# Forget-gate bias rows shifted once per block position, and score steps issued three ahead, in a gMLP and forgetting-attention trunk on Trainium2

## The chip, the cores and the metric

The kernel runs on one core of one Trainium2 chip. The metric is the device time of one launch in microseconds (us). The kernel before takes 2192.91 us, the median of three runs (2192.88 to 2193.39). TensorE (PE) does the matmuls, VectorE (DVE), ScalarE (ACT) and GpSimd (POOL) the elementwise work, and SyncE (SP) issues nearly all DMAs. Each engine works through its own instructions strictly in the order in which they were placed.

## The reference, cut to what matters

One gMLP layer, then one layer of forgetting attention with 12 heads over 1024 positions, each followed by a convolutional FFN. The change lies in the forgetting attention:

```python
f_logit = kvf[..., 2 * TOK_WIDTH:] + b_f
log_f_cum = jnp.cumsum(jax.nn.log_sigmoid(f_logit), axis=1)      # (b, s, 12)
...
for i in range(s // Q_BLOCK):                                    # Q_BLOCK = 128
    q0, q1 = i * Q_BLOCK, (i + 1) * Q_BLOCK
    logits = einsum("bqhd,bkhd->bhqk", q[:, q0:q1], k[:, :q1]) * scale
    decay = c[:, :, q0:q1, None] - c[:, :, None, :q1]
    logits = where(qpos >= kpos, logits + decay, -inf)
    p = softmax(logits)
    outs.append(einsum("bhqk,bkhd->bqhd", p, v[:, :q1]))
```

The term that depends on the query alone cancels in the softmax. The kernel therefore needs only the key term, one row of length 1024 per head, less any constant of the query block.

## The kernel before

Matrices are held as a high and a low part, and each product is three matmuls. The attention layer stands at about 1030 to 1440 us of the profiled execution.

**Steps.** The 48 steps are pairs of a head and a block position `jp` (0 to 3); a step has two query blocks of 128 (`a` = 0, 1) and looks at up to 256 x (`jp` + 1) keys. Heads come in pairs, in the order of `PSEQ` = 4, 5, 0, 1, 2, 3, eight steps for each pair. `s_tasks` makes a step's probabilities: it loads the head's row of cumulated log gates from DRAM (`cdram`), spread over 128 partitions, into a tile `nb` (three buffers); DVE takes the negative of one element (`ncq`, L1354); POOL adds it to the whole row (L1355) and adds the causal mask for the last 256 keys (`md`, L1357). PE multiplies queries and keys into a PSUM bank (`pa`), DVE adds the bias, writes the tile `P` and takes the minimum (L1381), ACT takes the exponential (L1387), DVE the reciprocal of the sum (L1388), POOL normalises (L459). `p_tasks` transposes the probabilities on PE into `pc` banks, splits them (ACT `PTh`, DVE `PTl`, L346 and L347), and multiplies them with V.

**Order.** `strict` pins every matmul to the order of the program. The loop over `t` merges `p_tasks` of step t with `s_tasks` of step t + `LOOK`, and puts between them matmuls of "fills": the K, Q and V projections of the next head pairs, each with a step by which it must be done. The rate at which fills are spent is the largest that any deadline asks for; the Q projections of the fourth and of the sixth pair (`PSEQ[3]`, `PSEQ[5]`) have the deadlines 8 x 2 + `KQD` = 21 and 8 x 4 + `KQD` = 37, as the K projections before them. What is left of a fill at its deadline is issued at once. Before the loop, `LOOK` steps of scores are issued, and then `PRE` (10000 ns of modelled PE time) of the first K projection.

**Banks and tiles.** `pa` has six PSUM banks, `pc` two. A score bank is free again when DVE has read it (L1381). A projection needs two `pa` banks from its first matmul to its evacuation. The tile `P` has six buffers, so three steps of two tiles fill them.

**Weights.** A weight block is loaded by SP into `wr` (L184, two buffers), multiplied by a norm's gain on DVE (L213), cast to its high part on ACT (`wh`, L217, two buffers), and its low part taken by POOL, or by DVE for the first four blocks (`wl`, L218). A new load waits until L218 has read the old block. After a Q projection, DVE scales each half of it (`qf`, L447), ACT casts (L429), DVE subtracts (L430), and SP copies the high and the low part to the other 64 partitions (L431, L432); a score matmul of that head pair needs these copies.

**The scan.** Just before the steps, DVE cumulates the log gates of all 12 heads (`cum`, L1532), and SP stores the 12 rows to `cdram` (L1533). The tag `nb`, with its three buffers, also serves `cum` and its two inputs `lf` and `zz`.

Of the kernel before, what the change touches and what calls it, by code (L numbers as in the profile page):

```python
# [10 lines left out]
F32 = mybir.dt.float32  # L11
F32R = mybir.dt.float32r
AF = mybir.ActivationFunctionType
ALU = mybir.AluOpType
AX = mybir.AxisListType

P = 128
D = 1024
S = 1024
# [9 lines left out]
QSCALE = -0.125  # L29
WIDE = 4 * 268  # L30
STRICT = True
LOOK = 2
VD = 11
LAG = 2
JORD = (1, 2, 3, 0)
# [24 lines left out]
def kernel(  # L60
# [33 lines left out]
    nc = tc.nc  # L94
# [6 lines left out]
    dp = ctx.enter_context(tc.tile_pool(name="dp", bufs=1, space=bass.MemoryType.DRAM))  # L101
# [6 lines left out]
    pbufs = [4]  # L108
# [4 lines left out]
    def nm(s):  # L113
        uid[0] += 1
        return f"{s}_{uid[0]}"
# [4 lines left out]
    def pa():  # L120
        return psA.tile([P, CH], F32, tag="pa", name=nm("pa"))
# [4 lines left out]
    def small(n, tag="sm", p=P):  # L126
        return sm.tile([P, n], F32, tag=tag, name=nm(tag))[:p]
# [8 lines left out]
    def mm(*a, **k):  # L136
        ins = nc.tensor.matmul(*a, **k)  # L137
        if strict[0]:
            tc.keep_in_program_order(ins)
        return ins  # L140
# [317 lines left out]
    def normalise(p, rinv):  # L458
        nc.gpsimd.tensor_scalar(p, p, rinv, 1.0, ALU.mult, ALU.mult)  # L459
# [57 lines left out]
    def drain(g):  # L517
        for _ in g:
            pass
# [465 lines left out]
    tp = tA.enter_context(tc.tile_pool(name="tA", bufs=2))  # L985
# [214 lines left out]
    tp = tF.enter_context(tc.tile_pool(name="tFa", bufs=4))  # L1200
# [67 lines left out]
    tp = tB.enter_context(tc.tile_pool(name="tB", bufs=2))  # L1268
# [1 line left out]
    otag[:] = ["nb", 3]  # L1270
    ptl[0] = 3
    t2b[0] = 2
    cdram = dp.tile([12, S], F32, name="cdram")
    odram = dp.tile([6 * P, S], F32, name="odram")
    strict[0] = STRICT
    w_q = b_w_q[0]
# [71 lines left out]
    def s_tasks(h, jp):  # L1348
        ks, dh, dl = (q[h % 2] for q in kq[h // 2])
        n2 = 256 * (jp + 1)  # L1350
        nb = tp.tile([P, S], F32, tag="nb", name=nm("nb"), bufs=3)
        nc.sync.dma_start(nb[:, :n2], cdram[h:h + 1, :n2].broadcast_to([P, n2]))
        ncq = small(1, "ncq")
        nc.vector.tensor_scalar(ncq, nb[:, n2 - 256:n2 - 255], -1.0, None, ALU.mult)  # L1354
        nc.gpsimd.tensor_scalar(nb[:, :n2], nb[:, :n2], 1.0, ncq, ALU.mult, ALU.add)  # L1355
        md = tp.tile([P, 2, P], F32, tag="md", name=nm("md"), bufs=1)
        nc.gpsimd.tensor_tensor(  # L1357
            md, nb[:, n2 - 256:n2].rearrange("p (a k) -> p a k", a=2), cmask, ALU.add)
        pts = []
        for a in range(2):  # L1360
            i = 2 * jp + a
            n = (i + 1) * P
            nd = n - P
            qs = slice(i * P, (i + 1) * P)
            p = tp.tile([P, S], F32, tag="P", name=nm("P"), bufs=pbufs[0])
            mn = None
            for k0 in range(0, n, CH):
                nn = min(CH, n - k0)
                nw = max(nn, 256)
                ps = pa()  # L1370
                mm(ps[:, :nw], dh[:, qs], ks[:, k0:k0 + nw], start=True, stop=False)
                mm(ps[:, :nw], dl[:, qs], ks[:, k0:k0 + nw], start=False, stop=True)
                e1 = min(k0 + nn, nd)
                parts = []
                if e1 > k0:
                    parts.append((k0, e1, nb[:, k0:e1]))
                if k0 + nn > nd:
                    parts.append((nd, n, md[:, a, :]))
                for c0, c1, bias in parts:
                    m2 = small(1)  # L1380
                    nc.vector.tensor_tensor_reduce(  # L1381
                        p[:, c0:c1], ps[:, c0 - k0:c1 - k0], bias, 1.0,
                        3.0e38 if mn is None else mn, ALU.add, ALU.min, m2)
                    mn = m2
                yield 2 * nw * 0.422
            rs, ri = small(1), small(1)
            nc.scalar.activation(p[:, :n], p[:, :n], AF.Exp, bias=mn, scale=-1.0, accum_out=rs)  # L1387
            nc.vector.reciprocal(ri, rs)  # L1388
            normalise(p[:, :n], ri)
            pts.append(p)  # L1390
        probs[h, jp] = pts
        if jp == final[h]:
            kq_free.extend(q[h % 2] for q in kq[h // 2])
# [64 lines left out]
    for pr in range(5):  # L1458
        p = PSEQ[pr + 1]
# [28 lines left out]
    H = 12  # L1488
# [41 lines left out]
        nc.scalar.copy(lf[:, b * CH:(b + 1) * CH], pt[:H])  # L1530
    cum = tp.tile([P, S], F32, tag="nb", name="cum", bufs=3)[:H]
    nc.vector.tensor_tensor_scan(cum, lf, zz, 0.0, ALU.add, ALU.add)  # L1532
    nc.sync.dma_start(cdram, cum)  # L1533
    wst.conv(wst.at["mv"] + 4)
    drain(mvg)
    mq = {}
# [25 lines left out]
    cost_of = [880 * (jp + 1) + 700 * (jp + 1) for _, jp in steps]  # L1562
    for t in range(LOOK):
        drain(s_tasks(*steps[t]))
# [4 lines left out]
    for t in range(48):  # L1569
        work, rate = -done, 0.0  # L1570
        for _, ns, _, d in fills:
            work += ns
            rate = max(rate, work / max(sum(cost_of[t:d]), 1))
        sg = s_tasks(*steps[t + LOOK]) if t + LOOK < 48 else iter(())
        pg = p_tasks(*steps[t])
        mg = itertools.islice(mem_g, MPER) if t >= MEMT else iter(())
        for cost in merge(pg, sg, mg):
            debt += cost * rate
            while debt > 0 and fills and fills[0][2] <= t:
                c = next(fills[0][0], None)  # L1580
                if c is None:
                    fills.pop(0)
                    done = 0.0
                else:
                    debt -= c
                    done += c
            if not fills or fills[0][2] > t:
                debt = 0.0
        while fills and fills[0][3] <= t + 1:
            drain(fills.pop(0)[0])  # L1590
            done = 0.0
        if t in (15, 31):
            pv_flush(0)
# [40 lines left out]
    tp = tF.enter_context(tc.tile_pool(name="tFb", bufs=4))  # L1634
# [60 lines left out]
```

## Time and profile before

| | |
|---|---|
| median of three runs | 2192.91 us |
| profiled execution | 2189.55 us |
| its span, first to last instruction | 2187.5 us |
| PE busy | 2121.6 us, 97% of the span |
| DVE busy | 1714.2 us, 78% |
| ACT busy | 1035.7 us, 47% |
| POOL busy | 785.1 us, 36% |
| mean granted TensorE clock | 0.993 |

PE is busy for nearly the whole span, so what counts are the places where it stands idle or runs at a lower granted clock. The chain of work that ended last has a share of 80% on PE. The shares are means over stages that differ: the attention layer is the part where PE idles most, and its stretches are to be read by themselves, by their idle time and by what ended it.

### The profile page before, as it was taken

How to read it: one execution, taken by the hardware profiler on the slowest of the kernel's cores; microseconds unless marked ns; L12 is line 12 of the kernel's file. 1: busy time of each engine (PE TensorE's matmuls, PEld its weight loads, DVE VectorE, ACT ScalarE, POOL GpSimd, SP SyncE). 2: the span in 40 equal slices, each digit the busy share in tenths (PEclk: the TensorE clock that was granted, in tenths of full speed). 3: DMA queues.
4: the chain of work that ended last, by engine and by line, in shares of the span. 5: the costliest groups of instructions: out<-in, count | busy, mean ns of one | idle time of the engine just before them, and what ended most of it. 6: DMA issues, size and time to landing. Idle time of an engine off the chain costs nothing.

```text
span 2187.5 us, 29468 instructions
## 1 busy us (share of the span) xinstructions
PE 2121.6 (97%) x10657; PEld 1784.9 (82%) x10657; DVE 1714.2 (78%) x2550; ACT 1035.7 (47%) x1732; POOL 785.1 (36%) x588
## 2 busy tenths in 40 slices
PE   8999999999999999999999999899999999999998
PEld 7998877888888888888788788778788888888886
DVE  4645658999999899676787776775899999988966
ACT  6562344444444434353565564764544444444433
POOL 2311443444444100231655554435344444420033
PEclk9999999999999999999999999999999999999999
DMA  5411231222222675622433333443222222267463
GB/s 179 104 30 30 77 106 60 87 87 87 87 78 78 224 279 179 202 103 75 121 88 89 91 94 87 115 158 105 70 87 87 78 78 86 78 218 259 148 203 116
DMA packets 221470, 251.94 MB, mean 115 GB/s; under 512 B 10330, under 2 KB 155904, under 8 KB 221324
## 3 DMA queue, kind: packets, MB, share of 16 engines
q1 hardware_dynamic: 220288, 249.62, 36.1%
q8 instruction: 84, 1.38, 0.3%
q10 hardware_dynamic: 1036, 0.43, 0.1%
q14 instruction: 62, 0.51, 0.1%
HBM read 196.49 MB, written 43.04 MB: 109 GB/s over the span
## 4 chain that ended last, share of the span: by engine, by line
PE 80%; DVE 8%; DMA 5%; ACT 4%; issue 2%; POOL 1%; SPq 0%; ACTq 0%; DVEq 0%; POOLq 0%
PE pa L137 72%; PE pc L137 5%; PE pc L143 2%; DMA nb<-cdram 1%; DVE P L1381 1%; DMA X<-xdram 1%; DVE X L347 1%; DMA ro<-hdram 1%; DVE X L430 1%; ACT P L1387 1%; DVE PTl L347 1%; DMA o<-odram 0%; ACT PTh L346 0%; ACT Pm L481 0%; DVE X L800 0%
## 5 line engine op out<-in xcount | busy, mean ns | idle before, releaser
L137 PE MATMUL pa<-X,wo 128*128 128x512 f32 x3696 | 841.9, 389 | 3.7 <-ACT X L346 2.5
L137 PEld LDWEIGHTS pa<-X,wo 128*128 128x128 f32 x3696 | 692.8, 188 | 150.3 <-ACT X L346 4.3
L137 PE MATMUL pa<-X,X 128*128 128x512 f32 (+2 forms) x1868 | 438.9, 378 | 6.9 <-DVE sm L1381 6.0
L137 PEld LDWEIGHTS pa<-X,X 128*128 128x128 f32 x1868 | 339.5, 189 | 75.5 <-DVE sm L1381 8.3
L137 PE MATMUL pa<-X,wh 128*128 128x512 f32 (+1 forms) x1216 | 352.8, 399 | 7.8 <-ACT wh L217 4.0
L641 POOL TENSOR_TENSOR wo<-raw,wo 128x512 fp32r<-128x512 f32 x132 | 210.5, 1595 | 203.9 <-ACT wo L639 176.6
L137 PEld LDWEIGHTS pa<-X,wh 128*128 128x128 f32 x1216 | 219.0, 189 | 53.9 <-ACT wh L217 4.5
L641 POOL TENSOR_TENSOR wo<-ws,wo 128x512 fp32r<-128x512 f32 x88 | 153.3, 1742 | 289.4 <-ACT wo L639 289.4
L799 ACT CAST X<-ro 128x1024 fp32r<-128x1024 f32 (+1 forms) x142 | 131.1, 964 | 173.9 <-DVE ro L807 68.9
L137 PE MATMUL pa<-X,wl 128*128 128x512 f32 (+1 forms) x608 | 194.1, 398 | 0.0
L639 ACT CAST wo<-ws 128x512 fp32r<-128x512 f32 x176 | 108.3, 617 | 176.3 <-PE pa L137 164.8
L639 ACT CAST wo<-raw 128x512 fp32r<-128x512 f32 x132 | 81.8, 620 | 184.9 <-PE pa L137 175.4
L137 PE MATMUL pa<-wh,X 128*128 128x256 f32 (+1 forms) x800 | 168.8, 289 | 0.1
L800 DVE TENSOR_TENSOR X<-ro,X 128x1024 fp32r<-128x1024 f32 (+1 forms) x124 | 145.0, 1198 | 30.4 <-ACT X L799 28.2
L800 POOL TENSOR_TENSOR X<-ro,X 128x1024 fp32r<-128x1024 f32 (+1 forms) x18 | 45.5, 2535 | 339.4 <-ACT X L799 336.6
L218 POOL TENSOR_TENSOR wl<-wr,wh 128x1024 fp32r<-128x1024 f32 (+1 forms) x41 | 103.4, 2522 | 175.0 <-ACT wh L217 175.0
L137 PEld LDWEIGHTS pa<-wh,X 128*128 128x128 f32 x800 | 133.3, 191 | 1.9 <-issue 0.2
L137 PEld LDWEIGHTS pa<-X,wl 128*128 128x128 f32 x608 | 110.3, 189 | 20.2 <-DVE wl L218 0.5
L137 PE MATMUL pa<-wl,X 128*128 128x256 f32 (+1 forms) x400 | 114.3, 286 | 4.4 <-POOL wl L218 3.6
L347 DVE TENSOR_TENSOR PTl<-pc,PTh 128x512 fp32r<-128x512 f32 (+1 forms) x152 | 90.8, 601 | 30.4 <-ACT PTh L346 28.6
L1387 ACT ACTIVATE P<-P,sm 128x128 f32<-128x128 f32 (+3 forms) x96 | 74.7, 778 | 73.9 <-DVE sm L1381 73.4
L459 POOL TENSOR_SCALAR P<-P,sm 128x128 f32<-128x128 f32 (+3 forms) x96 | 77.2, 806 | 86.7 <-DVE sm L1388 77.3
(195 smaller groups left out, 3312.7 us busy)
## 6 DMA issues: line engine op xcount, KB each, us to landing
ro<-hdram SPq DMA_DIRECT2D x67, 512.0 KB
raw<-in_a_ffn_in_dram SPq DMA_DIRECT2D x44, 512.0 KB
hdram<-X SPq DMA_DIRECT2D x44, 512.0 KB
raw<-in_b_ffn_in_dram SPq DMA_DIRECT2D x44, 512.0 KB
ro<-in_a_ffn_out_dram SPq DMA_DIRECT2D x35, 512.0 KB
ro<-in_b_ffn_out_dram SPq DMA_DIRECT2D x32, 512.0 KB
xdram<-X SPq DMA_DIRECT2D x24, 512.0 KB
X<-xdram SPq DMA_DIRECT2D x24, 512.0 KB
```

What stands on the lines that cost most here:

```text
L137: ins = nc.tensor.matmul(*a, **k)
L143: ins = nc.tensor.transpose(*a)
L218: eng.tensor_tensor(lo, raw, f32(hi), ALU.subtract)
L347: nc.vector.tensor_tensor(lo, src, f32(hi), ALU.subtract)
L430: nc.vector.tensor_tensor(dl[e][a, cs], qf[a], f32(dh[e][a, cs]), ALU.subtract)
L459: nc.gpsimd.tensor_scalar(p, p, rinv, 1.0, ALU.mult, ALU.mult)
L639: nc.scalar.copy(h, src)
L641: eng.tensor_tensor(l, src, f32(h), ALU.subtract)
L799: nc.scalar.copy(h, src)
L800: (nc.gpsimd if pool else nc.vector).tensor_tensor(l, src, f32(h), ALU.subtract)
L1381: nc.vector.tensor_tensor_reduce(p[:, c0:c1], ps[:, c0 - k0:c1 - k0], bias, 1.0, 3.0e38 if mn is None else mn, ALU.add, ALU.min, m2)
L1387: nc.scalar.activation(p[:, :n], p[:, :n], AF.Exp, bias=mn, scale=-1.0, accum_out=rs)
```

## The change

1. After the scan, DVE makes four tiles `cj`, one for each block position, with the 12 rows less their value at the first query of that position, and SP stores each to its own 12 rows of a `cdram` that is now 48 rows high. A step loads row 12 x `jp` + `h`, which is already shifted: `ncq` and POOL's addition to `nb` are gone, and `md` is made straight from the loaded row.
2. For `jp` = 0 and 1 the two query blocks' probabilities lie side by side in one tile `P`.
3. `LOOK` is 3: three steps of scores before the loop, and `s_tasks` of step t + 3 in the loop.

```diff
-LOOK = 2
+LOOK = 3
...
-    cdram = dp.tile([12, S], F32, name="cdram")
+    cdram = dp.tile([4 * 12, S], F32, name="cdram")
...
-        nc.sync.dma_start(nb[:, :n2], cdram[h:h + 1, :n2].broadcast_to([P, n2]))
-        ncq = small(1, "ncq")
-        nc.vector.tensor_scalar(ncq, nb[:, n2 - 256:n2 - 255], -1.0, None, ALU.mult)
-        nc.gpsimd.tensor_scalar(nb[:, :n2], nb[:, :n2], 1.0, ncq, ALU.mult, ALU.add)
+        r = 12 * jp + h
+        nc.sync.dma_start(nb[:, :n2], cdram[r:r + 1, :n2].broadcast_to([P, n2]))
...
+        both = None
+        if jp < 2:
+            both = tp.tile([P, S], F32, tag="P", name=nm("P"), bufs=pbufs[0])
         for a in range(2):
...
-            p = tp.tile([P, S], F32, tag="P", name=nm("P"), bufs=pbufs[0])
+            if both is None:
+                p = tp.tile([P, S], F32, tag="P", name=nm("P"), bufs=pbufs[0])
+            else:
+                p = both[:, a * (n - P):a * (n - P) + n]
...
-    nc.sync.dma_start(cdram, cum)
+    for jp in range(4):
+        n2 = 256 * (jp + 1)
+        cj = tp.tile([P, S], F32, tag="nb", name=nm("cj"), bufs=3)[:H, :n2]
+        nc.vector.tensor_scalar(cj, cum[:, :n2], cum[:, n2 - 256:n2 - 255], None, ALU.subtract)
+        nc.sync.dma_start(cdram[12 * jp:12 * jp + 12, :n2], cj)
```

Three places show how the change moves instructions. In the rows, "waits" names the engines or DMA queues on whose semaphores an instruction waits.

DVE from the scan on, before (`wr` are raw weights of the first K and Q projections, `L1381` rows read a score bank):

```order
L1532 SCALAR_TENSOR_TENSOR cum<-lf,zz 12x1024 [waits DVE_49,Activation_49,Pool_49]
L213 TENSOR_TENSOR wr_8395<-wr_8395,norms 128x1024 [waits DMAHW3_49]
L218 TENSOR_TENSOR wl_8594<-wr_8395,wh_8593 128x1024 [waits Activation_49]
L213 TENSOR_TENSOR wr_8397<-wr_8397,norms 128x1024 [waits DMAHW6_49]
L1354 TENSOR_SCALAR ncq_8606<-nb_8604 128x1 [waits DMAHW6_49]
```

The same place in the changed kernel:

```order
L1536 SCALAR_TENSOR_TENSOR cum<-lf,zz 12x1024 [waits DVE_49,Activation_49,Pool_49]
L1540 TENSOR_SCALAR cj_8591<-cum 12x256 [waits DVE_49]
L1540 TENSOR_SCALAR cj_8594<-cum 12x512
L1540 TENSOR_SCALAR cj_8597<-cum 12x768 [waits DMAHW5_49,DVE_49]
L1540 TENSOR_SCALAR cj_8600<-cum 12x1024 [waits DMAHW6_49,DVE_49]
L213 TENSOR_TENSOR wr_8395<-wr_8395,norms 128x1024 [waits DMAHW3_49]
```

Four instructions stand ahead of the first weight's gain, and the third and the fourth wait for a DMA: `cum` holds one of the three `nb` buffers, so they write into the buffers of the first two and wait for their stores.

PE before the loop, before (the last scores of the second step, then the first K projection, whose two banks are 8675 and 8676):

```order
L137 MATMUL pa_8656<-X_7994,X_8174 128x512 [waits PE_49]
L137 MATMUL pa_8656<-X_7994,X_8176 128x512
L137 MATMUL pa_8675<-X_7729,wh_8593 128x512 [waits PE_49,Activation_49]
L137 MATMUL pa_8676<-X_7729,wh_8593 128x512 [waits DVE_49]
L137 MATMUL pa_8675<-X_7730,wh_8593 128x512
```

The same place in the changed kernel (8676 to 8697 are the banks of the third step):

```order
L137 MATMUL pa_8659<-X_7994,X_8176 128x512
L137 MATMUL pa_8676<-X_7994,X_8174 128x512 [waits DMAHW5_49,PE_49,Activation_49]
L137 MATMUL pa_8676<-X_7994,X_8176 128x512 [waits DMAHW2_49]
L137 MATMUL pa_8681<-X_7994,X_8174 128x256 [waits DVE_49]
L137 MATMUL pa_8681<-X_7994,X_8176 128x256
L137 MATMUL pa_8692<-X_7994,X_8174 128x512 [waits DVE_49]
L137 MATMUL pa_8692<-X_7994,X_8176 128x512
L137 MATMUL pa_8697<-X_7994,X_8174 128x256 [waits DVE_49,PE_49]
L137 MATMUL pa_8697<-X_7994,X_8176 128x256
L137 MATMUL pa_8716<-X_7729,wh_8604 128x512 [waits DVE_49,PE_49,Activation_49]
L137 MATMUL pa_8717<-X_7729,wh_8604 128x512 [waits DVE_49,PE_49]
L137 MATMUL pa_8716<-X_7730,wh_8604 128x512
```

Eight score banks stand ahead of the K projection where there were four, and the projection's two banks now come from banks that DVE has to read first.

PE in the changed kernel where the fourth head pair begins (the last rows of its Q projection, 10739 and 10740, a transpose of `P` for another step, one pair of the next K projection, and the first scores of the pair, `pa_10896`):

```order
L137 MATMUL pa_10739<-X_7974,wl_10645 128x512
L137 MATMUL pa_10740<-X_7974,wl_10645 128x512
L143 MATMUL pc_10876<-ident,P_10490 128x128 [waits DVE_49,Pool_49]
L143 MATMUL pc_10876<-ident,P_10533 128x128 [waits Pool_49]
L143 MATMUL pc_10876<-ident,P_10490 128x128
L143 MATMUL pc_10876<-ident,P_10533 128x128
L137 MATMUL pa_10887<-X_7729,wh_10817 128x512
L137 MATMUL pa_10888<-X_7729,wh_10817 128x512 [waits DVE_49]
L137 MATMUL pa_10896<-X_8710,X_8176 128x384 [waits DMAHW2_49,PE_49,Activation_49]
L137 MATMUL pa_10896<-X_8710,X_8177 128x384 [waits DMAHW3_49,DVE_49]
```

SP at that place in the changed kernel (L431 and L432 are the copies of the Q projection):

```order
L1353 DMA nb_11106<-cdram 128x1024 [waits DMAHW7_49,DVE_49,Pool_49]
L1419 DMA odram<-os_10831 64x256 [waits DMAHW0_49,DVE_49]
L184 DMA wr_11158<-in_w_kv_dram 128x4x256 [waits DMAHW1_49,Pool_49]
L431 DMA X_8176<-X_8176 64x512 [waits DMAHW2_49,PE_49,Activation_49]
L432 DMA X_8177<-X_8177 64x512 [waits DMAHW3_49,DVE_49,PE_49]
```

Before, 48 matmuls and transposes stood between the end of this Q projection and these scores; now four transposes and two matmuls do. At the sixth pair both queues read the same way.

## Rows read from the trace of the kernel before

**Rows 1.** Windows: stretch, its length, busy us (and instructions) by engine, granted clock, DMA.
```profile
1050.00:1400.00 350.00, 328.21 (x2064) 286.40 (x2062) 258.00 (x802) 209.47 (x464) 189.04 (x198) 1.00 0.35 93
1400.00:1440.00 40.00, 29.60 (x171) 23.25 (x171) 30.81 (x63) 30.61 (x87) 12.53 (x27) 0.96 0.58 179
```

**Rows 2.** Waits of PE, 1050 to 1400: waiter, releaser, total us, times, longest.
```profile
PE pc L143 <- DVE PTl L347: 6.5, 6, 2.4
PE pa L137 <- DVE sm L1381: 4.8, 5, 2.1
PE pc L143 <- DVE sm L1388: 4.7, 4, 2.2
PE pc L143 <- POOL P L459: 2.2, 2, 1.8
PE pa L137 <- POOL wl L218: 1.9, 2, 1.1
```

**Rows 3.** Waits of PE, 1400 to 1440, the longest.
```profile
PE pa L137 <- DVE sm L1381: 3.3, 1, 3.3
```

**Rows 4.** Groups by line: instruction, count | busy us, mean ns | idle before, releasers.
```profile
L1354 DVE TENSOR_SCALAR ncq<-nb 128x1 f32<-128x1 f32 x48 | 7.0, 150 | 20.7 <-DMA nb<-cdram 20.4
...
L1355 POOL TENSOR_SCALAR nb<-nb,ncq 128x256 f32<-128x256 f32 (+3 forms) x48 | 46.7, 974 | 75.6 <-DVE ncq L1354 67.4 <-DVE sm L1388 7.6 <-issue 0.6
...
L430 DVE TENSOR_TENSOR X<-qf,X 64x512 fp32r<-64x512 f32 x26 | 27.5, 1059 | 0.7
```

**Rows 5.** Timeline of PE: its idle time behind the fourth and the sixth Q projection.
```profile
1216.38 0.52 PE L143 MATMUL pc<-ident,P 128*128 128x128 f32 x3 [2.37 <-DVE PTl L347]
...
1346.87 0.87 PE L143 MATMUL pc<-ident,P 128*128 128x128 f32 x4 [1.97 <-DVE sm L1388]
```

**Rows 6.** Timeline at the front: start, us, engine, line, operation [idle before <- releaser].
```profile
1034.71 1.19 DVE L213 TENSOR_TENSOR wr<-wr,norms 128x1024 f32<-128x1024 f32 x1
1034.81 0.33 SPq L1533 DMA_DIRECT2D cdram<-cum  x1
1036.71 0.83 SPq L1352 DMA_DIRECT2D nb<-cdram  x2
1037.08 1.26 PE L137 MATMUL pa<-X,wh 128*128 128x512 f32 x4 [4.03 <-ACT wh L217]
...
1040.59 0.15 DVE L1354 TENSOR_SCALAR ncq<-nb 128x1 f32<-128x1 f32 x1 [1.17 <-DMA nb<-cdram]
...
1049.15 0.35 DVE L1381 CUSTOM_DVE_ANT_0 P<-pa,md,sm 128x128 f32<-128x128 f32 x1
```

**Rows 7.** Timeline of SP and DVE: a weight load and the gain that waited for it.
```profile
1176.73 0.39 SPq L184 DMA_DIRECT2D wr<-in_w_kv_dram  x1
...
1181.44 1.60 DVE L213 TENSOR_TENSOR wr<-wr,norms 128x1024 f32<-128x1024 f32 x1 [0.83 <-DMA wr<-in_w_kv_dram]
```

**Rows 8.** Timeline of PE: a pair of score matmuls and the next instruction's start.
```profile
1050.85 0.63 PE L137 MATMUL pa<-X,X 128*128 128x512 f32 x2
1051.32 0.62 PE L137 MATMUL pa<-X,wh 128*128 128x512 f32 x2
```

**Rows 9.** Window at the front, columns as in rows 1: granted clock is 0.57.
```profile
1038.00:1042.00 4.00, 3.99 (x12) 2.90 (x11) 2.71 (x4) 2.33 (x2) 1.07 (x1) 0.57 0.87 153
```

**Rows 10.** Timeline where the sixth pair's Q projection ends.
```profile
1339.31 0.69 DVE L447 SCALAR_TENSOR_TENSOR qf<-pa,rb_b 128x512 f32<-128x512 f32 x1
1339.34 0.60 PE L143 MATMUL pc<-ident,P 128*128 128x128 f32 x4
...
1340.20 2.40 POOL L218 TENSOR_TENSOR wl<-wr,wh 128x1024 fp32r<-128x1024 f32 x1 [4.08 <-ACT wh L217]
...
1342.63 0.38 SPq L184 DMA_DIRECT2D wr<-in_b_w_out_dram  x1
...
1343.12 0.53 SPq L431 DMA_DIRECT2D X<-X  x1
...
1343.75 0.54 SPq L432 DMA_DIRECT2D X<-X  x1
```

## Prediction

> **What bounds the kernel now.** I read the windows of the attention stage first, then PE's waits in it, then the timeline at the places where the order moves. From 1050 to 1400 us PE is busy 328.2 of 350 us at full clock while DVE is busy 258 and POOL 189; from 1400 to 1440 it is busy 29.6 of 40 [rows 1]. The change leaves PE's work as it is, so it can win only PE's idle time: 21.8 us, then 10.4. That is not one bottleneck but many short stops, and PE's waits say which: for a transpose bank behind the split on DVE (6.5 us), for a score bank (4.8), for the reciprocal (4.7), for the normalised tile (2.2), for a weight's low part on POOL (1.9) [rows 2], and one of 3.3 us in the tail [rows 3]. Since every matmul is pinned, a matmul that comes too early in the order stops all behind it. That is the danger in issuing scores earlier.
>
> **What is taken away.** 48 `ncq` instructions, 7.0 us of DVE, with 20.7 us in which DVE stood before them for the loaded row, and 48 POOL additions, 46.7 us [rows 4]. Neither engine bounds the stage, so this counts only through PE's stops. A third step of lead gives the chain minimum, exponential, reciprocal, normalise one more step's time. I count as won: the score-bank waits but for the longest, 4.8 - 2.1 = 2.7 us; of the reciprocal waits the two short ones, 4.7 - 2.2 - 2.0 = 0.5 (the 1.97 is in rows 5); the normalise waits, 2.2; the low-part waits, 1.9, since POOL is freer [rows 2, 5]. Together 7.3 us. Not won are the stops of 2.0 to 2.4 us: they follow K and Q projections, where DVE's four subtractions (1059 ns each, L430, [rows 4]) hold up the splits, and the change does not move these. In the tail I take half of the 3.3 us, 1.5 [rows 3], as the last scores are issued a step earlier. Gain: 8.8 us; bounds 3.7 (the low parts and a third of the other 5.4) and 14.9 (the 7.3, the long stops of 2.1 and 2.2 us in rows 2, and all of the tail's 3.3).
>
> **The front, first cost.** (a) Between scan and first gain (L213, at 1034.71) stand four subtractions of 256 to 1024 elements on 12 partitions. The trace has none; the gain on 1024 elements took 1.19 us [rows 6], so I take 0.3, 0.5, 0.7 and 0.9 us by size, bounds half and all of 1.2 per 1024. The third waits for the first one's store. The store before was issued at 1034.81, and the load that waits for it at 1036.71, 1.9 us later [rows 6]. So: first done at 1035.0, store landed at 1037.0, third done at 1037.7, fourth at 1038.6; the first gain starts 3.9 us late. (b) The K projection starts at 1037.08, after an idle 4.03 us [rows 6]. In the new order eight score banks precede it, `pa` has six, and its two banks are those of the second step, free only when DVE has read them. Before, DVE had read the last of these at 1049.15 + 0.35 = 1049.50 [rows 6], which delayed nobody. On DVE two more gains stand inside that chain, and each waits for a weight load that can be issued only when an earlier L218 is done; such a load took 1176.73 to 1181.44, 4.7 us [rows 7]. Shifting the old chain by 3.9 us gives 1053.4. Going through the new order row by row from 1038.6 (gain, cast, low part and gain at 1.2 or a little less each, as the gain in rows 6; the first bank read by 1043.9; the next low part until 1045.5; the first load issued at 1042.0 and landed at 1046.7; gain and three reads of 0.35 us or a little more until 1049.3; the second load issued at 1045.5 and landed at 1050.2; gain and two reads) gives 1052.3; with loads that cost nothing it would be 1051. I take 1052.3. (c) So the K projection starts 15.2 us later. PE has by then done the third step's four score banks, which counts back: a 512-column pair takes 1051.32 - 1050.85 = 0.47 us [rows 8], two such and two of half the size make 1.4. The front costs 13.8 us, bounds 12 and 15.5. Nothing hides it, since the fills, PE's cover, are queued behind. The restart at half clock is paid in both kernels: 0.57 over 4 us, 1.7 us lost [rows 9].
>
> **The fourth and sixth head pair, second cost.** Scores of step t + 3 need the pair's Q copies at t = 21 and 37, the very steps at which that Q projection must be done, and these two fills set the rate, so they end on their deadline. Before there was a step between. Take the sixth pair's end as clock zero (1339.31). Four transposes and a matmul pair, about 0.9 us, are all that PE now has before the scores. The copies went out at +3.8 and +4.4 (1343.12, 1343.75), because SP first issued a weight load (1342.63) that waits for POOL's low part (1340.20 + 2.40) [rows 10]. In the new order a load stands ahead of the copies at both pairs. For their landing, the store of 48 KB took 1.9 us and the first row's load of 128 KB, into as many bytes as a copy, 3.8 to DVE's release at 1040.59 [rows 6]; I take 3.0, between them, as the copies have the longer one's size but read no DRAM. Copies there at +7.4, PE stops for 6.5 us, bounds 5.4 and 7.3. Behind the idle 4.03 us the granted clock was at its lower level of 1.2 GHz for some 3 us, which cost 1.7 us [rows 9]; I add that to each. Against it stand the stops already there, 2.37 and 1.97 us [rows 5], which the longer one swallows, and 1.7 us for the one that had fallen to the lower clock already. Sum: 2 x 8.2 - 6.0 = 10.4 us, bounds 8.2 and 12.0. Nothing in the order fills the stop; the cover was 48 matmuls and transposes.
>
> The shared tile for `jp` 0 and 1 makes four steps in a row need six `P` tiles, seven at three of the changes of head. A seventh waits on DVE for transposes two PE pieces later, so I cost it at nothing; its cover is the three steps of lead, and without it I bound each by the longest score-bank wait, 2.1 us [rows 2].
>
> **Sum.** 13.8 + 10.4 - 8.8 = +15.4 us. The profiled execution took 2189.55 us; it lies 3.4 us under the median, and I apply the difference to the median: 2192.91 + 15.4 = 2208.3 us.
>
> **Rivals.**
> - Q copies in time (0.13): the load ahead of them finds its buffer free, and the scores wait no longer than rows 5 show. For: at the fourth pair the old order had no load there. Against: the new order has, behind the same POOL instruction. 13.8 - 8.8 = +5.0, 2197.9.
> - No front stop (0.08): the K projection finds free banks. Against: six banks, eight tiles ahead. 10.4 - 8.8 = +1.6, 2194.5: the change does little beyond moving waits.
> - Faster (0.05): POOL's 46.7 us and DVE's 27.7 us gone end the long stops too. DVE's subtractions at 1059 ns against 690 for a scaling of twice the partitions [rows 4, 10] look disturbed; if POOL's additions are what disturbs them, all of PE's idle time goes, 21.8 + 10.4 us [rows 1] and two spells at the lower clock, 3.4: 35.6 us. Against it the lower bounds, 12.0 at the front and 2 x 5.4 at the pairs, 22.8: -12.8, 2180.1. It decides once over 22.8 us are won. Against: the instruction beside the long subtractions is POOL's low part (L218), which stays.
> - Dearer (0.12): upper bounds and little gain: 15.5 + 12.0 - 3.7 = +23.8, 2216.7.
>
> By the Trainium skill (SBUF — State Buffer, Who interferes with whom), a VectorE instruction with two SBUF inputs and a GpSimd instruction that reads SBUF block each other, the later one until the earlier ends. By that rule the faster rival's 35.6 us could not all come from POOL's additions, since L218 reads SBUF too; the trace agrees as far as L430's 1059 ns [rows 4] go, and I leave that rival at 0.05.
>
> **How the numbers follow.** Forecast 0.62, own range 2200 to 2216: its bounds all together would give 12.0 + 8.2 - 14.9 = +5.3 and +23.8, but they need not fall together. A measurement of this kernel tells about 0.2%, 4.4 us, from no change. Faster: the faster rival, 0.05. Same: no front stop (0.08) and some of copies in time (0.05), 0.13. Slower: 0.82. The range 2197 to 2218 leaves out no front stop and faster, 0.13, and a little of each edge.
>
> **What would show it.** Right: PE idle for 13 us or more between the last scores and the first K matmul, broken by the third step's scores, with the K projection near 1052; a PE wait on a DMA X<-X of 5 us and more at the fourth and sixth pair, then a granted clock of half for some 3 us; normalise waits nearly gone; POOL 47 us less busy. Wrong: a K start before 1045, pairs without a wait on the copies, or stops behind K projections that shrink below 1 us.

## The result and the profile after

The changed kernel takes 2211.39 us, the median of four runs (2209.49 to 2213.63); the kernel before, measured with it, takes 2192.89 us. The ratio is 1.010, 95% interval 1.0086 to 1.0114. The change makes the kernel slower by 18.5 us; 15.4 were forecast.

The head of the page of the changed kernel's profile, its span and the engines' busy time:

```profile
span 2209.9 us, 29350 instructions
...
PE 2126.8 (96%) x10657; PEld 1792.0 (81%) x10657; DVE 1711.1 (77%) x2506; ACT 1033.8 (47%) x1732; POOL 736.9 (33%) x540
```

The span is 22.4 us longer than in the profiled execution of the kernel before. PE has the same 10657 matmuls. It is busy for 5.2 us more (2121.6 before) and idle for 17.2 us more (2209.9 - 2126.8 = 83.1 against 65.9). POOL has lost 48 us, as the change says, and the kernel is still slower: what was added to PE's waits is larger.

PE's waits from 1044 us to 1440 us (waiter, releaser, total us, times, longest) answer to [rows 2, 3]; the changed kernel's steps end some 20 us later than those of the kernel before, so its tail is in part behind this stretch:

```profile
PE pa L137 <- DVE sm L1385: 19.6, 9, 9.9
PE pa L137 <- DMA X<-X: 15.7, 2, 7.9
PE pc L143 <- DVE PTl L347: 7.8, 10, 2.0
PE pa L137 <- ACT Pm L481: 2.9, 1, 2.9
PE pa L137 <- POOL wl L218: 1.1, 2, 0.8
```

Two lines hold nearly all that is new: score banks behind DVE's reads (L1385), of which most lies at the front, and two waits of a score matmul on the copies of Q (`X<-X`). The waits on the reciprocal (4.7 us in [rows 2]) and on the normalised tile (2.2) are gone, the low part's have fallen from 1.9 to 1.1.

**The front.** DVE's and SP's timeline from the scan on (start, us, engine, line, operation, idle before):

```profile
1034.60 0.74 DVE L1540 TENSOR_SCALAR cj<-cum 12x256 f32<-12x256 f32 x2
1036.45 1.33 DVE L1540 TENSOR_SCALAR cj<-cum 12x768 f32<-12x768 f32 x2 [1.12 <-DMA cdram<-cj]
1037.71 1.21 DVE L213 TENSOR_TENSOR wr<-wr,norms 128x1024 f32<-128x1024 f32 x1
...
1041.34 0.38 SPq L184 DMA_DIRECT2D wr<-in_w_kv_dram  x1
...
1045.86 1.36 DVE L213 TENSOR_TENSOR wr<-wr,norms 128x1024 f32<-128x1024 f32 x1
```

The first gain starts at 1037.71, against 1034.71 in [rows 6]. The third subtraction did wait for a store. The third gain, of a weight block whose load went out at 1041.34, starts at 1045.86, 4.5 us later, and DVE's score reads stand around it. PE's idle places there, from its timeline:

```profile
1043.41 1.22 PE L137 MATMUL pa<-X,X 128*128 128x512 f32 x2 [9.89 <-DVE sm L1385]
1047.64 0.77 PE L137 MATMUL pa<-X,X 128*128 128x256 f32 x2 [3.00 <-DVE sm L1385]
1049.36 0.77 PE L137 MATMUL pa<-X,wh 128*128 128x512 f32 x1 [0.95 <-DVE sm L1385]
1051.43 1.62 PE L137 MATMUL pa<-X,wh 128*128 128x512 f32 x3 [1.30 <-DVE sm L1385]
```

PE waits for a bank four times, 15.1 us in all against 4.03 before. The first two waits are of the third step's scores, the last two of the K projection's two banks, which start at 1049.36 and 1051.43.

**The fourth and the sixth pair.** SP's rows at the fourth pair, then PE's idle places at both:

```profile
1223.16 0.38 SPq L184 DMA_DIRECT2D wr<-in_w_kv_dram  x1
1223.66 0.48 SPq L431 DMA_DIRECT2D X<-X  x1
1224.25 0.53 SPq L432 DMA_DIRECT2D X<-X  x1
...
1228.80 1.09 PE L137 MATMUL pa<-X,X 128*128 128x384 f32 x2 [7.83 <-DMA X<-X]
...
1365.09 1.17 PE L137 MATMUL pa<-X,X 128*128 128x384 f32 x2 [7.91 <-DMA X<-X]
```

These are scores that wait 7.8 and 7.9 us for copies. Before, there were stops of 2.37 and 1.97 us on transposes at these two places [rows 5].

**The clock.** Windows of PE (stretch, length, busy us, granted clock, DMA):

```profile
1043.40:1054.00 10.60, 5.33 (x11) 0.50 0.64 197
...
1260.00:1270.00 10.00, 10.00 (x52) 0.83 0.34 100
1360.00:1370.00 10.00, 4.91 (x18) 0.66 0.68 158
1400.00:1410.00 10.00, 10.00 (x55) 0.83 0.43 113
```

A value between 0.5 and 1 means that the clock changed level inside the window. The lower level (1.2 GHz) is met at the front, behind both long waits (0.86 from 1230 to 1240 behind the first of them), and also near 1260 and 1400, behind stops of 2.1 and 2.0 us, and behind one of 2.9 us at 1425 (0.86 and 0.79 in the two windows from 1420 to 1440).

These windows are of one execution, and the order of the matmuls does not settle the clock. Two of the kernels below, look2 and look2_cj, have their matmuls in the same order, and in both PE stops for 2.4 us up to the same transpose at 1105.64. Behind it the clock fell in the first and not in the second:

```profile
1106.00:1110.00 4.00, 4.00 (x17) 0.61 0.07 16
```

```profile
1106.00:1110.00 4.00, 4.00 (x26) 1.00 0.07 16
```

### The profile page after: what moved, and what is told of

It is laid out like the page before. It is cut to its first block, busy times and chain, and to the rows that moved or that the text cites. A ratio compares the mean times of both kernels' runs of the same rounds, so it can differ in the third digit from the quotient of the medians.

```text
span 2209.9 us, 29350 instructions
## 1 busy us (share of the span) xinstructions
PE 2126.8 (96%) x10657; PEld 1792.0 (81%) x10657; DVE 1711.1 (77%) x2506; ACT 1033.8 (47%) x1732; POOL 736.9 (33%) x540
## 4 chain that ended last, share of the span: by engine, by line
PE 86%; DVE 6%; ACT 4%; DMA 2%; issue 1%; POOL 1%; ACTq 0%; DVEq 0%; SPq 0%; POOLq 0%
PE pa L137 78%; PE pc L137 5%; PE pc L143 3%; DVE X L347 1%; DVE P L1385 1%; ACT P L1391 1%; DVE wr L213 1%; DMA X<-X 0%; DMA o<-odram 0%; ACT X L429 0%; ACT wh L217 0%; DVE td L594 0%; DVE PTl L347 0%; DVE X L430 0%; POOL wl L218 0%
## 5 line engine op out<-in xcount | busy, mean ns | idle before, releaser
L218 POOL TENSOR_TENSOR wl<-wr,wh 128x1024 fp32r<-128x1024 f32 (+1 forms) x41 | 103.3, 2522 | 197.7 <-ACT wh L217 182.8
```

What stands on the lines that cost most here:

```text
L218: eng.tensor_tensor(lo, raw, f32(hi), ALU.subtract)
```

## The experiments

On the chips of these runs the kernel before takes 2189.3 to 2190.3 us in the median, so kernels are compared by their ratio to it; 0.001 is 2.2 us. The changed kernel is at 1.010, some 22 us.

**look2: the third step taken back.**

```diff
-LOOK = 3
+LOOK = 2
```

> The changed kernel with LOOK back at 2: shifted rows and shared tile alone. Theory (the loss comes from the third step's place in the order, at the front and at the two pairs): no wait on X<-X at the fourth and sixth pair, two steps of scores before the loop, K projection near 1040 us (3.0 us later than before, the four subtractions), less about 2.5 us of gain from a freer POOL: about 2193.4 us, 2191 to 2196. Rival (the shifted rows themselves cost: longer rows of DRAM, the stores, the shared tile): 2198 us or more, spread over the steps.

Measured: 0.9995 (0.9985 to 1.0005). No wait on `X<-X` is left. PE's idle time ahead of the K projection:

```profile
1038.60 2.08 PE L137 MATMUL pa<-X,wh 128*128 128x512 f32 x4 [7.26 <-ACT wh L217]
```

It is 7.26 us against 4.03 [rows 6], the 3.0 us of the subtractions and little else. By the ratio the kernel is 1.1 us faster than before, where 0.5 slower was expected; the interval includes no change at all. The shifted rows and the shared tile do not cost anything that can be measured; all of the loss comes with the third step.

**third_behind: the third step of scores behind the first 10 us of K projection.**

```diff
-    for t in range(LOOK):
+    for t in range(2):
         drain(s_tasks(*steps[t]))
     grow(3, 2)
...
     while done < PRE:
         done += next(fills[0][0])
+    for t in range(2, LOOK):
+        drain(s_tasks(*steps[t]))
```

> The changed kernel with two steps of scores before the loop, then the 10 us of K projection, then the third step of scores; the loop is unchanged. Theory (six banks, eight tiles ahead of the projection): the K projection starts near 1040 us instead of 1049 to 1051, the front costs 3 us instead of 13, the pairs' waits stay at 7.8 us: about 2201 us, 2199 to 2204. Rival (the front is late because of the subtractions and the weight loads on DVE, whatever the banks): K projection still at 1046 or later, 2207 us or more.

Measured: 1.0076 (1.0061 to 1.0091), some 5 us less than the changed kernel where 7 to 12 were expected. PE's idle places at the front:

```profile
1040.53 2.07 PE L137 MATMUL pa<-X,wh 128*128 128x512 f32 x4 [7.26 <-ACT wh L217]
1058.24 0.62 PE L137 MATMUL pa<-X,X 128*128 128x384 f32 x2 [0.54 <-DVE sm L1385]
1060.79 0.73 PE L137 MATMUL pa<-X,X 128*128 128x512 f32 x2 [1.47 <-DVE sm L1385]
1063.52 1.19 PE L137 MATMUL pa<-X,X 128*128 128x512 f32 x2 [1.53 <-DVE sm L1385]
```

The projection starts at 1040.53, so the front stop was made by the banks, as the theory says. Half of what that won was given back: the third step's banks are now wanted while the projection holds two of the six, which costs 3.5 us in three waits, and a spell at the lower clock follows (the windows 1062 to 1066 and 1066 to 1070 show 0.55 and 0.60).

**q_early: K and Q due one step earlier.**

```diff
-KQD = 5
+KQD = 4
```

> The changed kernel with every K and Q fill due one step earlier (KQD 4 for 5). Theory (the Q fill ends exactly where the three-ahead scores need its copies): both waits on X<-X of 7.8 and 7.9 us gone, stops of about 2 us behind the Q projections back, the front unchanged: 10 to 14 us less than the changed kernel, about 2199 us. Rival (the copies are late whenever the pair begins, since loads stand ahead of them): waits of 3 us or more remain, 2205 us or more. Open beside: whether the two spells at the lower clock near 1260 and 1400 go too (3.4 us).

Measured: 1.0052 (1.0033 to 1.0070), 10.5 us less than the changed kernel by the ratios. The time is as expected, the picture is not: the waits have shrunk and not gone.

```profile
1223.02 0.41 PE L137 MATMUL pa<-X,X 128*128 128x384 f32 x1 [2.92 <-DMA X<-X]
...
1353.55 1.28 PE L137 MATMUL pa<-X,X 128*128 128x384 f32 x2 [6.15 <-DMA X<-X]
```

Between the end of the Q projection (1214.09 + 0.62 = 1214.71) and the stop (1220.10) PE now has 5.4 us of work; at the sixth pair (1344.27 to 1347.40) only 3.1 us. The step gained is one whose scores are of `jp` 0, the shortest. A step is no fixed time: at the fourth pair matmuls of the next projection are spread through it, at the sixth a single pair is. That waits of 3 us and more remain was the rival's mark at the sixth pair; its reason, that loads stand ahead of the copies, is taken up by load_behind.

**both_mended: both edits.** The diffs are those of third_behind and q_early.

> Both edits together: third step behind the first 10 us of K projection, and K and Q due one step earlier. Theory (the two costs are apart and add): 2187 to 2191 us, by 22 to 24 us under the changed kernel and a little under the kernel before. Rival (the freed time is taken back by later stops, the gain of three steps' lead being nothing): 2193 us or more.

Measured: 1.0032 (1.0019 to 1.0045). The two gains do add: 0.0024 and 0.0048 taken from 0.0100 leave 0.0028. But the sum doesn't come down to the kernel before, so the rival's time is right.

**load_behind: the changed kernel with the weight loads behind the copies.** Copies and later loads of the two pairs are pinned in the order of the program:

```diff
-            nc.sync.dma_start(f32(dh[e][b, cs]), f32(dh[e][a, cs]))
-            nc.sync.dma_start(f32(dl[e][b, cs]), f32(dl[e][a, cs]))
+            for d in (dh, dl):
+                ins = nc.sync.dma_start(f32(d[e][b, cs]), f32(d[e][a, cs]))
+                if cpin[0]:
+                    tc.keep_in_program_order(ins)
...
+        late = key in (("q", PSEQ[3]), ("q", PSEQ[5]))
+        cpin[0] = late
         yield from evac_q_g(tp, ps, rb, qs[0:2], qs[2:4])
+        cpin[0] = False
+        dpin[0] = late
```

> The changed kernel with the weight loads that stood ahead of the Q copies of the fourth and sixth pair issued behind them; no other engine's work is moved on purpose. The copies needed 4.6 us from issue to PE's start in the changed kernel. Theory (the load's 512 KB shares the queues with the copies): they land in about 2.5 us, each wait on X<-X falls from 7.8 to 5 or 5.5 us, 4 to 6 us less than the changed kernel, about 2206 us. Rival (the copies take that long by themselves, the load ahead costs only its 0.5 us of issue): waits of 7.2 us or more, 2210 us or more.

Measured: 1.0072 (1.0057 to 1.0086), 6 us less than the changed kernel. SP and PE at the fourth pair:

```profile
1217.58 0.48 SPq L433 DMA_DIRECT2D X<-X  x1
...
1219.78 0.48 SPq L433 DMA_DIRECT2D X<-X  x1
...
1224.15 1.19 SPq L185 DMA_DIRECT2D wr<-in_w_kv_dram  x2
...
1219.91 0.41 PE L137 MATMUL pa<-X,X 128*128 128x384 f32 x1 [3.21 <-DMA X<-X]
1222.17 0.66 PE L137 MATMUL pa<-X,X 128*128 128x384 f32 x1 [1.85 <-DMA X<-X]
```

The first score matmul starts 2.3 us after the first copy is issued, and the wait is 3.21 + 1.85 = 5.1 us in place of 7.8 (3.21 + 1.43 at the sixth pair). In the changed kernel it started 1228.80 - 1223.66 = 5.1 us after the first copy's issue. The second copy, which the second matmul needs, was issued 4.0 us behind the end of the Q projection (at 1215.80), hardly sooner than the 4.2 us of the changed kernel, but its matmul started 2.4 us after it and not 4.6 or more. So the 512 KB of the load, which went out just ahead, held the copies up on their way; the load's delay of their issue counts for the first copy (1.8 us behind the projection, 3.6 in the changed kernel) and little for the second. The 5 us that remain are DVE's and SP's chain and the copies' own flight.

**q_two_early: both_mended with K and Q due two steps earlier.**

```diff
-KQD = 4
+KQD = 3
```

> As both_mended, but K and Q due two steps earlier than in the changed kernel (KQD 3). There the waits on X<-X were still 2.96 and 5.76 us, as the one step gained is a short one (jp 0). Theory (a second, longer step covers the rest): both waits gone, and the spells at the lower clock behind them, 8 to 11 us less than both_mended: 2185 to 2188 us with the kernel before at 2189.6. Rival (the stop moves to another place, since the same fills then leave later steps bare): 2192 us or more.

Measured: 1.0020 (1.0009 to 1.0031). Both waits on the copies are gone, 8.7 us of idle time, yet the kernel gained only 2.6 us. The rival's time is right, and the stops did move: waits on POOL's low part, which were 0.3 us in both_mended, are 3.1 us here, those on splits 9.6 for 7.0, and a stop of 2.73 us on a split stands about where the sixth pair's copies were waited for. That the fills pulled forward are what left these places bare is the likely reason; no run shows it by itself.

**look2_cj: look2 with the last two subtractions behind the first gain.**

```diff
-    for jp in range(4):
+    def shift(jps):
+        for jp in jps:
...
+    shift((0, 1))
     wst.conv(wst.at["mv"] + 4)
+    shift((2, 3))
     drain(mvg)
```

> As look2, but with only the first two subtractions ahead of the first weight's gain and the other two behind it. Theory (the subtractions' wait for their stores delays the gain and with it the K projection): the first K matmul starts 2 to 2.5 us earlier than in look2, where PE idled 7.3 us ahead of it, and the kernel is 2 us faster than look2: 0.998 to 0.999 of the kernel before. Rival (another chain holds the projection): idle of 6.5 us or more, no difference.

Measured: 2184.40 us, 0.9980 (0.9969 to 0.9991). PE's idle time ahead of the projection is 4.83 us for 7.26, so the subtractions held up the gain, as the theory says:

```profile
1036.26 2.07 PE L137 MATMUL pa<-X,wh 128*128 128x512 f32 x4 [4.83 <-ACT wh L217]
```

In time it is 3.3 us below look2 by the ratios, which are from two chips and whose intervals overlap a little.

**q_two_cj: q_two_early with the same edit.**

> As q_two_early, with the later two subtractions behind the first gain as in look2_cj. Theory (the costs are apart and add): 1 to 2.5 us less than q_two_early. Rival (three steps' lead needs those rows sooner): no difference or more.

Measured: 1.0013 (1.0002 to 1.0023), 1.5 us less than q_two_early, with intervals that overlap. Against look2_cj, which has two steps of lead, the third step with all its found costs moved is still 0.0033 slower, about 7 us. PE's waits from 1044 to 1440, first of q_two_cj:

```profile
PE pc L143 <- DVE PTl L347: 9.6, 10, 2.7
PE pa L137 <- DVE sm L1385: 6.8, 14, 1.9
PE pc L143 <- ACT PD L1440: 3.2, 2, 2.3
PE pa L137 <- POOL wl L218: 3.1, 4, 1.7
PE pa L137 <- ACT Pm L481: 2.9, 1, 2.9
```

and of look2_cj, run again as look2_cj_again:

```profile
PE pa L137 <- DVE sm L1385: 9.8, 6, 3.4
PE pc L143 <- DVE PTl L347: 7.0, 7, 2.4
PE pc L143 <- DVE sm L1392: 4.4, 3, 2.2
PE pc L143 <- ACT PD L1440: 2.0, 2, 1.6
PE pc L143 <- POOL P L459: 1.5, 1, 1.5
```

With the third step the waits on reciprocal and normalised tile (4.4 + 1.5) are gone and the score banks' are 3.0 us less; in their place stand 2.6 us more on splits, 3.1 on low parts, 2.9 on the tail's exponentials and 1.2 on `PD`. What the longer lead wins in one chain it hands to the next. All waits of this stretch together are 28.3 us against 27.4, so the list holds no more than about 1 of the 7 us.

**look2_pool: where the gain comes from.** Each loaded row gets a column of zeros added by POOL, about as long a piece of work as the addition that the change removed (43.6 us in all, for 46.7 in [rows 4]):

```diff
+        nc.gpsimd.tensor_scalar(nb[:, :n2], nb[:, :n2], 1.0, nought, ALU.mult, ALU.add)
         md = tp.tile([P, 2, P], F32, tag="md", name=nm("md"), bufs=1)
```

> look2_cj with POOL adding a column of zeros to each loaded row, 48 additions as long as those that the change took away (46.7 us of POOL in the kernel before), before md is made; results stay the same. In look2 PE's waits from 1044 to 1440 us were 26.8 us against 31.2 in the kernel before, with no third step. Theory (those 4.4 us come from POOL's freed time): the waits on POOL's low part (1.9 us in the kernel before) and on normalised tiles come back, 3 to 5 us more than look2_cj. Rival (they come from the row's shorter way, ncq and the wait of DVE for it): less than 1.5 us more.

> look2_cj once more, on the same chip as look2_pool, for a comparison of the two on one chip: 0.998 of the kernel before, as it was there (0.9969 to 0.9991). If it were only noise that made it faster, 1.000.

Measured on one chip: look2_pool 2194.05 us, 1.0018 (1.0006 to 1.0029); look2_cj_again 2185.23 us, 0.9973 (0.9961 to 0.9985). POOL's additions cost 8.8 us, more than the 3 to 5 expected, and look2_cj's lead over the kernel before stands. PE's waits from 1044 to 1440 grew by 7.0 us. Of what the theory named, the waits on low parts came to 0.6 us only and those on normalised tiles from 1.5 to 2.9; the rest is with score banks (2.3 more), splits (1.3) and reciprocals (1.2). The long stops behind projections grew. PE, first in look2_cj_again, then in look2_pool:

```profile
1108.31 0.55 PE L143 MATMUL pc<-ident,P 128*128 128x128 f32 x3 [2.36 <-DVE PTl L347]
1153.33 0.55 PE L143 MATMUL pc<-ident,P 128*128 128x128 f32 x3 [1.50 <-POOL P L459]
```

```profile
1106.41 0.90 PE L143 MATMUL pc<-ident,P 128*128 128x128 f32 x3 [3.14 <-DVE PTl L347]
1156.43 0.60 PE L143 MATMUL pc<-ident,P 128*128 128x128 f32 x3 [2.88 <-POOL P L459]
```

DVE's subtractions behind the projections, grouped by line (count | busy us, mean ns | idle before), in the same order:

```profile
L430 DVE TENSOR_TENSOR X<-qf,X 64x512 fp32r<-64x512 f32 x28 | 28.2, 1006 | 0.8
...
L424 DVE TENSOR_TENSOR X<-kf,X 64x512 fp32r<-64x512 f32 x10 | 7.9, 789 | 0.3
```

```profile
L430 DVE TENSOR_TENSOR X<-qf,X 64x512 fp32r<-64x512 f32 x28 | 31.6, 1128 | 0.8
...
L424 DVE TENSOR_TENSOR X<-kf,X 64x512 fp32r<-64x512 f32 x10 | 12.1, 1212 | 0.3
```

The same instructions take 12% and 54% longer beside a busier POOL (the third kind, L423, does not: 1258 and 1224 ns; nor do the splits of 128x512, which read one of their inputs from PSUM: 686 ns in both), and the split that PE waits for is queued behind them on DVE (a third such stop, near 1218 and 1223 us, grew from 2.31 to 2.90 us). By the Trainium skill (SBUF — State Buffer, Who interferes with whom), a VectorE instruction with both inputs in SBUF contends with a GpSimd instruction that reads SBUF; the means of L430 and L424 agree with it, that of L423 does not show it.

This is what additions on POOL can do, but the change did not gain by it: in the kernel before, with its own 48 additions, the same two rows are:

```profile
L430 DVE TENSOR_TENSOR X<-qf,X 64x512 fp32r<-64x512 f32 x28 | 28.9, 1032 | 0.8
...
L424 DVE TENSOR_TENSOR X<-kf,X 64x512 fp32r<-64x512 f32 x10 | 8.3, 826 | 0.3
```

All three kinds together took 48.8 us there, 48.7 in look2_cj_again and 55.9 in look2_pool. The old additions waited for `ncq`; the experiment's start as soon as the row has landed, and so fall at other times. They also lengthen the row's way to the scores, which is what the rival named. So look2_pool does not decide between theory and rival, and its 8.8 us are no measure of what the change won. The gain itself is look2_cj's 4 to 6 us (0.0020 and 0.0027).

## Why the prediction held, step by step

The time lies inside the range, 3.1 us above the forecast, and each of the two costs stands where it was put. The sizes are off by more than the sum shows. The comparison below is of the two profiled executions, 22.4 us apart and so 7.0 above the forecast; before's lies 3.4 us under its median, which is most of the difference to the 18.5. That the medians came within 3.1 us is in part luck: the terms were off to both sides.

- **Front, forecast 13.8.** The first gain was late by 3.0, not 3.9 us: the first two subtractions took 0.74 us together and the store landed sooner. The K projection's banks started at 1049.36 and 1051.43, forecast 1052.3. Idle time rose by 15.1 - 4.0 = 11.1 us. The cause, eight tiles ahead of six banks, is shown by third_behind, where the projection starts at 1040.53. The step that failed is "the restart at half clock is paid in both kernels": in the new order 5.33 us of busy time up to 1054, broken by the stops, ran at 0.50, and the window from 1054 to 1058 still shows 0.84; before, it was 3.99 us at 0.57 [rows 9].
- **Pairs, forecast 10.4.** The projection at the fourth pair ended at 1219.45 + 0.62 = 1220.07; the copies were issued 3.6 and 4.2 us later, forecast 3.8 and 4.4. The term that was mis-sized is the landing: 3.0 was taken, between a store of 48 KB and the first row's load, and it took 4.6 us from the second copy's issue to PE's start, because of the weight load ahead. The trace of before had the row for it, the 4.7 us of such a load [rows 7], which I set against the front alone. I counted the load ahead of the copies as a delay of their issue; load_behind shows that for the second copy, which is waited for last, its bytes are the larger part (2.2 us, against 0.2 of issue). Idle time: 7.83 + 7.91 - 2.37 - 1.97 = 11.4 us, where 2 x 6.5 - 4.3 = 8.7 was meant.
- **Gain, forecast 8.8.** Outside these places idle time fell by 11.1 + 11.4 - 17.2 = 5.3 us. The normalise waits went, as forecast (2.2), and of the reciprocal waits 2.7 where 0.5 was counted. Three terms were too large. In the tail, for which I took 1.5, the wait of 3.3 us [rows 3] became one of 2.9 on the exponential `Pm` (L481), and PE is idle for 11.0 us of 47 there in both kernels (1398 to 1445 before, 1420 to 1467 after): nothing was won. Of the score-bank waits, for which I took 2.7, 2.4 us are still there beside the front and the longest (19.6 - 15.1 - 2.1). Of the low parts 0.8 of 1.9 was won. And splits, for which I had no term, were waited for 5.9 us up to the tail, against 4.1 before without the 2.37 of the fourth pair. Where the gain comes from stays open: look2 has as much of it without the third step (waits of 26.8 us from 1044 to 1440, for some 31 before), but look2_pool does not show that it is POOL's freed time. q_two_cj against look2_cj shows that the third step adds nothing to it.
- **Clock, forecast 1.7.** PE's busy time rose by 5.2 us with the same matmuls. The stops near 1257 and 1397, of 2.1 and 2.0 us, were each followed by a spell at the lower level, as was the 2.9 us at 1425; before, of the stops behind projections only that at 1346.87 was. I had no term for stops that are there in both kernels and now end in a lower clock. How much of the 5.2 us belongs to the change is not shown: PE was busy for 2117.5 us in the profiled execution of look2_cj and for 2121.2 in that of look2_cj_again, the same kernel, and behind the same stop the clock fell in look2 and not in look2_cj.

So 11.1 + 11.4 - 5.3 + 5.2 = 22.4. Against the forecast the front was 2.7 us cheaper in idle time, the pairs 2.7 dearer, the clock 3.5 dearer and the gain 3.5 smaller.

**The rivals.** Copies in time and no front stop are refuted by the rows above. Faster asked whether POOL's additions are what disturbs DVE's subtractions. Additions on POOL can (look2_pool), but taking the old ones away shortened L430 only from 1032 to 1006 ns, and the stops of 2.3 to 2.4 us stay in look2_cj_again. That L218 is what still lengthens the subtractions there is what I set against this rival; no run took it away. The four marks of the prediction came true: PE idle for 15 us at the front, waits of over 5 us on `X<-X` with a lower clock behind, normalise waits gone, POOL 48 us less busy. Of the rival that is dearer, its smaller gain came true in part (5.3, where the forecast had 8.8 and this rival 3.7), its upper bound at the front did not.

**Left open.** Why the third step stays 7 us slower when no score waits for its copies and the front stop is gone is not known. The waits of its steps are only about 1 us longer in sum, and no run took those that grew away one by one. What makes the clock fall behind a stop in one execution and not in another is open too, so the spells near 1260 and 1400 cannot be put down to the long waits ahead of them.

**A kernel that beats both.** look2_cj: shifted rows, two steps of lead, and the last two subtractions behind the first gain. It takes 0.9980 and 0.9973 of the kernel before in two sets of runs, 4 to 6 us less than that and some 27 us less than the changed kernel.

## What to carry to other kernels

In an order that is pinned, a longer lead is paid wherever something ends on a deadline or runs out of buffers: list those places (here the first projection's banks and the copies of Q), and measure the cover in the work that stands there, since a step that is short covers little. A transfer that the next step waits for should be issued ahead of large loads, whose bytes delay it more than their issue does. Work put on an engine that is hardly waited for can still cost, when it runs beside instructions of the waited-for engine: 48 additions on POOL cost 8.8 us. Shifting the rows once was worth 4 to 6 us here, for a reason that is not shown, and the lead that came with it was worth less than nothing. And a term for the clock is to be read from more than one execution.

## What was not expected of the hardware

PE started 2.3 us after the issue of a 128 KB copy inside SBUF with no load ahead of it, and 5.1 us after it with a 512 KB load just ahead. DVE's subtraction L424 of 64x512 took 789 ns in the mean in one kernel and 1212 ns in one that differs by 48 additions on POOL. Behind a stop of 2.4 us that two kernels have at the same time and the same place in the order, the granted clock was 0.61 for 4 us in one (look2) and 1.00 in the other (look2_cj).
